# An opening on un-normed x: norms computed beside the products, unread products on TensorE, and a reordered set of loads

## The chip, the cores and the metric

The kernel runs on one core of a Trainium2 chip. The core has five engines that run side by side, each with its own queue of instructions: TensorE (PE in the profile; it multiplies and transposes), VectorE (DVE), ScalarE (ACT), GpSimd (POOL) and SyncE (SP, which here only issues transfers). ACT and POOL can issue transfers too. Sixteen DMA engines carry all transfers. The metric is the device time of one execution in microseconds (us).

## The reference

The reference is one decoder layer on x of 512 tokens by 2048 channels, all in float32:

```
h    = x * rsqrt(mean(x^2) + eps) * g_pre                    # RMSNorm per token
[q | k | v | z_att | u | g_glu | z_conv] = h @ w_in          # 2048 x 7168
A: 8 heads of stick-breaking attention on q, k, v, times silu(z_att)
B: u * sigmoid(g_glu) -> causal depthwise conv (31 taps) -> LayerNorm -> silu
   -> @ w_pw2, times silu(z_conv)
out  = x + RMSNorm(concat(A, B) @ w_out) * g_post
```

Only the first two lines concern the change: the norm of x, and the first 512 of the columns g_glu of the product h @ w_in, which the kernel computes first.

## The kernel before, in words

**Split numbers.** Every float32 operand of a product is split into hi (rounded to the format TensorE multiplies in) and lo (the rest), and a product is made of three: hi x hi, hi x lo, lo x hi. ACT makes hi (`AF.Copy`), DVE makes lo by a subtraction (`split`, lines 99 to 103). A split of a weight block of 128 x 2048 elements takes one ACT and one DVE instruction; in the opening the blocks are split in four parts of 512 columns (`part`).

**The opening** makes the first 512 columns of g_glu by rows: the output is four tiles `ps0[m]` (128 tokens each), and the sum over 2048 channels goes in four groups kg of 512 channels. So there are 16 blocks (kg, m), numbered n = 4 kg + m, each of twelve products of 128 x 512 (`rows_block`, lines 448 to 462; the last four, on line 460, use the low part of x). A block needs the weight group kg (`w0[kg]`, loaded by `load_w0`, hi and lo) and the transposed x tile (m, kg). `turn_x` transposes a tile of x on TensorE (line 244), ACT copies hi out of PSUM (line 248), DVE subtracts lo (line 251), and ACT copies the raw transposed values (line 255, or 250 for kg 0), which later steps use.

**The norm before.** For kg 0 x is used un-normed, with g_pre's 512 factors multiplied into the weight rows; after these blocks `scale_up` multiplies each `ps0[m]` by its token's root. For kg 1 to 3 `scale_x` multiplies x by root and g_pre on DVE (line 231) before it is transposed. For that, g_pre is spread over the 128 partitions by `broadcast_g`: three pairs of products with the constant `pick` (lines 168, 169), each copied to SBUF by DVE. The sums of squares are made by ACT and DVE (`square`), the roots by ACT's Ln and Exp and a Newton step on DVE. The transposed copies of kg 0 are normed at the end by `norm_first`: the roots are spread by four transpositions (`broadcast_roots`), and four steps multiply 512 columns each and split them again.

**The order of work.** In the opening the order on PE, DVE and ACT is written out by hand: the dictionary `plan` lists for each block n (slot n in the text) what is issued ahead of the block and behind it. Transfers on SP and POOL are placed by the planner of the framework, in order of the program's priorities; an instruction that waits holds up those behind it on its queue. A buffer of the pools `raws`, `his` and `los` exists twice, so the third weight group is loaded when the first one's raw tile has been split.

**After the opening** come steps of 1024 x 256 weights, two per pair of 128 output columns: first u (here in the order second half, first half of the channels), then q, k, then v. `stream` loads the raw weights on SP (line 311) and splits them. After u's first step `turn_gates` transposes the four kept row tiles (`keep_rows`) of g_glu on PE, and ACT applies the sigmoid. v is computed by a scheme with seven instead of eight products, for which weight blocks are added in DRAM: `v_sum`, 16 transfers of 1 MB on POOL's queue (lines 484 and 488), from DRAM to DRAM, of which `sum_next` releases one after each block from 5 on and then one after each unit of a step, in order; a sum also waits for the transfer whose result it reads. The depthwise convolution runs on DVE in the background from u's first step on.

Of the kernel before, what the change touches and what calls it, by code (L numbers as in the profile page):

```python
# [48 lines left out]
def hybrid_layer(  # L49
# [81 lines left out]
    pick = const.tile([4, 4, P], F32R, name="pick")  # L131
    for j in range(4):
        nc.gpsimd.tensor_copy(pick[:, j, :], ident[:4, j : j + 1].to_broadcast([4, P]))
# [15 lines left out]
    g_ks = early.tile([4, P], F32, name="g_ks")  # L149
    g_col = const.tile([P, 4], F32, name="g_col")  # L150
    g_rows = t2("g_rows")[:4]
    g_bc = {}

    def turn_g():

        ps = trp.tile([P, S], F32, tag="tr", name="g_col_ps")
        nc.tensor.transpose(ps[:, :4], g_ks, ident[:4, :4])
        nc.vector.tensor_copy(g_col, ps[:, :4])

    def split_g():  # L160
        g_parts = [t2(f"g_{part}", F32R)[:4] for part in ("hi", "lo")]
        split(*g_parts, g_rows)
        return g_parts

    def broadcast_g(j, g_hi, g_lo):

        ps = trp.tile([P, S], F32, tag="tr", name=f"g_ps{j}")
        nc.tensor.matmul(ps, pick[:, j, :], g_hi, start=True, stop=False)
        nc.tensor.matmul(ps, pick[:, j, :], g_lo, start=False, stop=True)
        g_bc[j] = t2(f"g_bc{j}")  # L170
        nc.vector.tensor_copy(g_bc[j], ps)
# [28 lines left out]

    def square(m, j, eng=None):
        junk = t2(f"junk{m}_{j}")
        total = sums[m][:, j : j + 1]
        if eng is None:
            nc.scalar.activation(junk, xts[m][j], AF.Square, accum_out=total)
        else:
            eng.tensor_tensor_reduce(
                out=junk, in0=xts[m][j], in1=xts[m][j], scale=1.0, scalar=0.0,
                op0=ALU.mult, op1=ALU.add, accum_out=total,
            )  # L210
# [3 lines left out]
    def root_table(m):  # L214
# [6 lines left out]
        rsqrt_table(y, v)  # L221
        roots[m] = y, v

# [15 lines left out]
    def turn_x(m, j):  # L239
# [8 lines left out]
        nc.scalar.activation(hi, src, AF.Copy)  # L248
        if j == 0:
            nc.scalar.copy(raw_h[m, 0], src)  # L250
        nc.vector.tensor_tensor(out=lo, in0=src, in1=f32(hi), op=ALU.subtract)

        def keep_raw():
            raw_h[m, j] = t2(f"xw{m}_{j}").rearrange("p (i t) -> p i t", i=4)
# [22 lines left out]
    def norm_first():  # L277

        lo = {}
        for i in range(5):  # L280
            if i < 4:
                x, hi = whole[:, i, :], h_hi[0][:, i, :]
                nc.vector.scalar_tensor_tensor(
                    out=x, in0=x, scalar=g_col[:, i : i + 1], in1=rbc[0],
                    op0=ALU.mult, op1=ALU.mult,
                )
                nc.scalar.activation(hi, x, AF.Copy)
            if i > 0:
                nc.vector.tensor_tensor(
                    out=h_lo[0][:, i - 1, :], in0=whole[:, i - 1, :], in1=f32(h_hi[0][:, i - 1, :]),  # L290
                    op=ALU.subtract,
                )
# [40 lines left out]
    def pair(c0, post, name, halves=(0, 1)):  # L333
# [3 lines left out]
        def unit(half, i):  # L337
            def go(w):
                hi, lo = w
                if half == halves[0]:  # L340
                    ps[i] = mm(f"{name}_{i}")
                cs = slice(i * P, (i + 1) * P)
                for k in range(8):
                    mm3(
                        ps[i], (hi[:, k, cs], lo[:, k, cs]), h_at(half * 8 + k),
                        half == halves[0] and k == 0, half == halves[1] and k == 7,
                    )
                if half == halves[1]:
# [3 lines left out]
        for half in halves:  # L352
# [658 lines left out]
    def conv_in(t):  # L1011
        if t > 1:
            pair(C_G + t * 256, post_g(2 * t), f"g{t}")

        pair(C_U + t * 256, post_u(2 * t), f"u{t}", (0, 1) if t else (1, 0))
# [31 lines left out]
    with tc.manual_schedule(engines={mybir.EngineType.DVE, mybir.EngineType.Activation}):  # L1047
# [5 lines left out]
        def load_w0(kg, eng=nc.sync):  # L1053
            raw, hi, lo = (
                raws.tile([P, 4, S], F32, tag="raw", name=f"r_gn{kg}"),
                his.tile([P, 4, S], F32R, tag="hi", name=f"h_gn{kg}"),
# [210 lines left out]
```

## Time and profile before

| what | value |
|---|---|
| three runs | 877.31 to 878.13 us, median 877.72 us |
| the profiled execution | 880.52 us, its span 878.8 us |
| granted TensorE clock, mean | 0.992 of full |
| PE busy | 856.1 us, 97% of the span |
| DVE / ACT / POOL busy | 625.1 / 391.5 / 123.8 us |
| moved by DMA | 163.32 MB, mean 186 GB/s |

The profile shows one execution. A line such as "start, duration, engine, line, operation, out<-in, shape" is one instruction or several alike in a row (xN); in brackets behind it stands how long the engine had been idle and what released it. PE's matmuls overlap, so the distance from one start to the next is what one costs. In tables of stretches the columns after the time are the busy time of PE, PE's weight loads, DVE, ACT and POOL with their counts, then the granted clock of TensorE, the mean busy share of the DMA engines and their GB/s.

### The profile page before, as it was taken

To read this page: it belongs to the slowest core of one execution; us is meant where nothing else is said; L and a number is where in the kernel's file an instruction comes from. 1 tells how busy PE (TensorE), PEld (TensorE's weight loads), DVE (VectorE), ACT (ScalarE), POOL (GpSimd) and SP (SyncE) were. 2 spreads that over 40 slices of the span, in tenths; PEclk is the share of its full clock that TensorE was granted. 3 is DMA by queue.
4 is the path that set the end of the run, shared out by engine and by line. 5 is a ranking of instruction groups with operands and counts; after the bars stand their busy time and mean duration, and the time that the engine had idled before them with its cause. 6 is when DMAs were issued, how large, how long until landed. Compare 5 with 4: busy or idle time off the path is not lost.

```text
span 878.8 us, 9764 instructions
## 1 busy us (share of the span) xinstructions
PE 856.1 (97%) x3879; PEld 708.3 (81%) x3879; DVE 625.1 (71%) x744; ACT 391.5 (45%) x446; POOL 123.8 (14%) x156
## 2 busy tenths in 40 slices
PE   6899989999999999999999999999999999999995
PEld 4688868888888888888888888888888888888884
DVE  5766877996598987969697994226533676458775
ACT  5653323645434454334432535325823346456543
POOL 0011110001122042213111143122001000000031
PEclk9999989999999999999999999999999999999998
DMA  8499984557776655885477656772233246556783
GB/s 300 160 268 275 290 201 142 192 191 268 247 156 152 183 178 135 186 202 197 156 142 165 192 172 159 166 182 90 78 117 99 96 148 242 193 196 244 290 282 103
DMA packets 87406, 163.32 MB, mean 186 GB/s; under 512 B 2994, under 2 KB 52406, under 8 KB 83584
## 3 DMA queue, kind: packets, MB, share of 16 engines
q1 hardware_dynamic: 70176, 110.92, 37.5%
q0 software_dynamic: 16320, 50.33, 25.2%
q10 hardware_dynamic: 864, 1.44, 0.5%
q8 instruction: 30, 0.49, 0.2%
q14 instruction: 16, 0.13, 0.0%
HBM read 158.49 MB, written 54.53 MB: 242 GB/s over the span
## 4 chain that ended last, share of the span: by engine, by line
PE 89%; DMA 6%; DVE 2%; ACT 2%; issue 0%; DVEq 0%; SPq 0%; ACTq 0%
PE k L328 3%; PE k L326 3%; PE k L327 3%; PE za L327 3%; PE za L326 3%; PE za L328 3%; PE zc L327 3%; PE zc L328 3%; PE a L922 3%; PE a L923 3%; PE zc L326 3%; PE a L924 3%; DMA r_q<-in_w_in_dram 3%; DMA r_k<-in_w_in_dram 3%; PE q L328 2%; PE u L327 2%
## 5 line engine op out<-in xcount | busy, mean ns | idle before, releaser
L383 DVE SCALAR_TENSOR_TENSOR acc<-hg,vec,acc 128x512 f32<-128x512 f32 x240 | 182.3, 759 | 6.9
L100 DVE TENSOR_TENSOR l_w<-r_w,h_w 128x2048 fp32r<-128x2048 f32 x28 | 64.1, 2291 | 42.5 <-ACT h_w L99 42.5
L99 ACT ACTIVATE h_w<-r_w 128x2048 fp32r<-128x2048 f32 x28 | 53.5, 1915 | 42.7 <-DMA r_w<-ws 12.6
L328 PE MATMUL k<-h_hi,l_k 128*128 128x512 f32 x128 | 51.2, 400 | 1.6 <-DVE l_k L100 1.6
L326 PE MATMUL k<-h_hi,h_k 128*128 128x512 f32 x128 | 51.2, 400 | 1.4 <-ACT h_k L99 1.4
L327 PE MATMUL k<-h_lo,h_k 128*128 128x512 f32 x128 | 50.8, 397 | 0.0
L326 PE MATMUL u<-h_hi,h_u 128*128 128x512 f32 x128 | 50.2, 392 | 0.0
L326 PE MATMUL q<-h_hi,h_q 128*128 128x512 f32 x128 | 50.1, 391 | 0.0
L326 PE MATMUL za<-h_hi,h_za 128*128 128x512 f32 x128 | 49.9, 390 | 0.0
L328 PE MATMUL u<-h_hi,l_u 128*128 128x512 f32 x128 | 49.9, 390 | 0.0
L326 PE MATMUL zc<-h_hi,h_zc 128*128 128x512 f32 x128 | 49.9, 390 | 0.0
L328 PE MATMUL q<-h_hi,l_q 128*128 128x512 f32 x128 | 49.9, 390 | 0.0
L327 PE MATMUL u<-h_lo,h_u 128*128 128x512 f32 x128 | 49.9, 390 | 0.0
L327 PE MATMUL q<-h_lo,h_q 128*128 128x512 f32 x128 | 49.9, 390 | 0.0
L328 PE MATMUL za<-h_hi,l_za 128*128 128x512 f32 x128 | 49.8, 389 | 0.0
L327 PE MATMUL za<-h_lo,h_za 128*128 128x512 f32 x128 | 49.8, 389 | 0.0
L328 PE MATMUL zc<-h_hi,l_zc 128*128 128x512 f32 x128 | 49.8, 389 | 0.0
L327 PE MATMUL zc<-h_lo,h_zc 128*128 128x512 f32 x128 | 49.8, 389 | 0.0
L922 PE MATMUL a<-h_w,f_hi 128*128 128x512 f32 x128 | 49.8, 389 | 0.0
L923 PE MATMUL a<-l_w,f_hi 128*128 128x512 f32 x128 | 49.8, 389 | 0.0
L924 PE MATMUL a<-h_w,f_lo 128*128 128x512 f32 x128 | 49.8, 389 | 0.0
L653 POOL TENSOR_SCALAR_AFFINE_SELECT t<-t 128x128 f32<-128x128 f32 x64 | 35.6, 635 | 81.9 <-DVE t L676 48.9
(339 smaller groups left out, 2118.4 us busy)
## 6 DMA issues: line engine op xcount, KB each, us to landing
ws<-in_w_out_dram POOLq DMA_DIRECT2D x24, 1024.0 KB, 9.3
r_w<-ws SPq DMA_DIRECT2D x16, 1024.0 KB
vs<-in_w_in_dram POOLq DMA_DIRECT2D x12, 1024.0 KB, 13.2
r_w<-in_w_out_dram SPq DMA_DIRECT2D x12, 1024.0 KB
r_u<-in_w_in_dram SPq DMA_DIRECT2D x8, 1024.0 KB
r_q<-in_w_in_dram SPq DMA_DIRECT2D x8, 1024.0 KB
r_k<-in_w_in_dram SPq DMA_DIRECT2D x8, 1024.0 KB
r_v<-vs SPq DMA_DIRECT2D x8, 1024.0 KB
```

Source lines behind the costliest of these rows:

```text
L99: nc.scalar.activation(hi, src, AF.Copy)
L100: nc.vector.tensor_tensor(out=lo, in0=src, in1=f32(hi), op=ALU.subtract)
L326: nc.tensor.matmul(ps, wh, ah, start=first, stop=False)
L327: nc.tensor.matmul(ps, wh, al, start=False, stop=False)
L328: latest[0] = nc.tensor.matmul(ps, wl, ah, start=False, stop=last).ins
L383: bgq.append(lambda j=j: nc.vector.scalar_tensor_tensor(out=acc, in0=hg[:, j : j + S], scalar=vec[:, ct, j : j + 1], in1=acc, op0=ALU.mult ...
L653: nc.gpsimd.affine_select(out=blk, in_=blk, compare_op=ALU.is_gt, fill=0.0, base=0, pattern=[[-1, P]], channel_multiplier=1,)
L922: nc.tensor.matmul(ps, fh[:, kk, ts], hi[:, k, :], start=st, stop=False, skip_group_check=True)
L923: nc.tensor.matmul(ps, fh[:, kk, ts], lo[:, k, :], start=False, stop=False, skip_group_check=True)
L924: nc.tensor.matmul(ps, fl[:, kk, ts], hi[:, k, :], start=False, stop=en, skip_group_check=True)
```

## The change

1. *Un-normed x for three groups.* kg 0, 1 and 2 use x as loaded; `g_col` now holds 1536 factors of g_pre (12 x 128 instead of 4 x 128, loaded on ACT's queue), and `part` multiplies them into the weight rows for kg < 3. Only kg 3 is still scaled ahead of its transposition. `scale_up` moves from after group 0 to after group 2. Three of the four spreads of g_pre by products fall away with `pick`, `split_g` and `broadcast_g`; the last 512 factors come spread by one transfer (`load_g(3)`).
2. *Norms beside the products.* Squares, roots and their spread move to slots 1 to 9. `norm_first` now norms three groups of raw copies: group 1 (four tiles of 128 tokens, four multiplications of 128 columns each), group 0 (four multiplications of 512 columns), group 2 (as group 1), each item followed by ACT's hi and DVE's lo; 14 calls instead of 5.
3. *Unread products.* 10 products of a constant into an unread tile before `turn_g`, 3 after it, 8 between the transpositions of the first tile and block 0.
4. *First tile.* For tile (0, 0) hi is copied by DVE instead of ACT, and its lo comes after the four weight parts.
5. *Loads.* The rows of the first weight group are issued on SP, between the x tiles, instead of on ACT's queue; then x by columns; the third and fourth weight group on POOL's queue (slots 3 and 4) instead of SP's; the convolution's vectors at slot 6 instead of 10.
6. *The end.* u's first step is split in slot 13 instead of 12, the second one right after the fourth of the last calls of `norm_first`; u's halves come in the order first, second, with the channels of each half taken from its fifth group of 128 on. `turn_gates` moves ahead of u's first step and takes its 16 transpositions token tile by token tile.

```
+    def root_sum(m):
...
-        nc.scalar.activation(hi, src, AF.Copy)
-        if j == 0:
-            nc.scalar.copy(raw_h[m, 0], src)
-        nc.vector.tensor_tensor(out=lo, in0=src, in1=f32(hi), op=ALU.subtract)
+        if (m, j) == (0, 0):
+            nc.vector.tensor_copy(hi, src)
+        else:
+            nc.scalar.activation(hi, src, AF.Copy)
+            nc.vector.tensor_tensor(out=lo, in0=src, in1=f32(hi), op=ALU.subtract)
...
+        def norm(x, i, ts):
+            nc.vector.scalar_tensor_tensor(
+                out=x, in0=x, scalar=g_col[:, i : i + 1], in1=rbc[0][:, ts],
+                op0=ALU.mult, op1=ALU.mult,
+            )
+        def by_tokens(j, m):
+            x, ts = raw_h[m, j], slice(m * P, (m + 1) * P)
+            for i in range(4):
+                norm(x[:, i, :], 4 * j + i, ts)
+            return h_hi[j][:, :, ts], h_lo[j][:, :, ts], x
+        def by_channels(j, i):
+            x = whole[:, i, :]
+            norm(x, i, slice(0, S))
+            return h_hi[j][:, i, :], h_lo[j][:, i, :], x
+        todo = [(f, j, n) for j, f in ((1, by_tokens), (0, by_channels), (2, by_tokens)) for n in range(4)]
...
+                    k = n if c0 != C_U else (n + 4) % 8
...
-            split(hi[:, i], lo[:, i], raw[:, i], g_col[:, i : i + 1] if kg == 0 else None)
+            k = kg * 4 + i
+            split(hi[:, i], lo[:, i], raw[:, i], g_col[:, k : k + 1] if kg < 3 else None)
...
-        nc.sync.dma_start(g_ks, g_pre[: 4 * P].rearrange("(k p) -> k p", p=P))
+        nc.scalar.dma_start(g_ks, g_pre[: 12 * P].rearrange("(k p) -> k p", p=P))
         load_x(0, 0)
-        load_w0(0, nc.scalar)
-        nc.sync.dma_start(g_rows, g_pre.rearrange("(j c) -> j c", j=4))
-        for m in range(1, NT):
-            load_x(m, 0)
-        load_x(0, 1, 2, 3)
-        load_x(1, 1, 2, 3)
+        load_w0_rows(0)
+        load_w0_rows(1)
+        load_x(1, 0)
+        load_w0_rows(2)
+        load_w0_rows(3)
+        load_x(2, 0)
+        load_x(3, 0)
+        for m in range(NT):
+            load_x(m, 1)
         load_w0(1)
-        load_x(2, 1, 2, 3)
-        load_x(3, 1, 2, 3)
+        for m in range(NT):
+            load_x(m, 2, 3)
+        load_g(3)
+        def idle_products(count):
+            for i in range(count):
+                nc.tensor.matmul(idle[:, :P], mean_w, mean_w, start=True, stop=True)
+        idle_products(10)
         turn_g()
+        idle_products(3)
...
+            1: [do(square, 0, 0), do(square, 2, 0, dve), do(square, 1, 0), do(square, 3, 0, dve)],
+            2: [do(part, 1, 0), do(part, 1, 1), do(square, 0, 1), do(square, 1, 1, dve)],
+            3: [
+                do(load_w0, 2, nc.gpsimd), do(part, 1, 2), do(part, 1, 3),
+                do(square, 2, 1), do(square, 3, 1, dve),
+            ],
...
+            9: [
+                do(part, 3, 1), broadcast_roots, do(scale_block, 12), do(scale_up, 0),
+            ],
+            10: [do(part, 3, 2), do(scale_block, 13), do(scale_up, 1), do(next, first)],
+            11: [do(part, 3, 3), do(scale_block, 14), do(scale_up, 2), do(next, first)],
+            12: [do(scale_block, 15), do(next, first), do(scale_up, 3), do(next, first)],
+            13: [lambda: loaded.update({0: steps[0].load()}), do(keep_rows, 0)],
+            14: [do(keep_rows, 1), do(next, first), do(next, first)],
+            15: [do(keep_rows, 2), do(next, first)],
         turn_block(0)
+        idle_products(8)
         for i in range(4):
             part(0, i)
-        turn_block(1)
-        for m in range(NT):
-            square(m, 0, dve)
+        keeps[0]()
...
         keep_rows(3)
-        next(first)
-        next(first)
+        for _ in range(4):
+            next(first)
+        loaded[1] = steps[1].load()
+        for _ in first:
+            pass
```

More of the change, by code (lines that the diff above doesn't have):

```diff
@@ L156, in turn_g, with load_g @@
         ps = trp.tile([P, S], F32, tag="tr", name="g_col_ps")
[L157 to L169, printed above, removed]
+        nc.tensor.transpose(ps[:, :12], g_ks, ident[:12, :12])
+        nc.vector.tensor_copy(g_col, ps[:, :12])
+    def load_g(j):
         g_bc[j] = t2(f"g_bc{j}")
-        nc.vector.tensor_copy(g_bc[j], ps)
+        nc.sync.dma_start(g_bc[j], g_pre[j * S : (j + 1) * S].partition_broadcast(P))
     NV = TAPS + 4
@@ L1222, in hybrid_layer @@
             sum_next(sumq)
-        if n + 1 < len(steps):
+        if n + 1 < len(steps) and n + 1 not in loaded:
             loaded[n + 1] = steps[n + 1].load()
@@ L1228, in hybrid_layer @@
             sum_next(v_sumq)
-            if n == 0 and unit is step.units[-1]:
-                turn_gates()
             if n == 0 and unit is step.units[0]:
```

184 lines of the change are left out of this document (84 added, 100 removed).

## The prediction, on record before the result

> **What bounds the kernel now.** I read the page first, then TensorE's waits, then the opening in order of time, then stretches of the transfers.
>
> ```profile
> span 878.8 us, 9764 instructions
> PE 856.1 (97%) x3879; PEld 708.3 (81%) x3879; DVE 625.1 (71%) x744; ACT 391.5 (45%) x446; POOL 123.8 (14%) x156
> ```
>
> TensorE (PE) bounds the kernel, so a change can only pay where PE is idle or at half clock. The view of PE's waits names those places, in total us, number and longest.
>
> ```profile
> PE xT L244 <- DMA x<-in_x_dram: 5.0, 2, 3.6
> PE g_col_ps L157 <- POOL pick L133: 2.3, 1, 2.3
> PE xT L244 <- DVE x L231: 2.1, 2, 1.3
> PE k L328 <- DVE l_k L100: 1.6, 1, 1.6
> PE k L326 <- ACT h_k L99: 1.4, 1, 1.4
> PE g_ps L169 <- DVE g_lo L100: 1.1, 1, 1.1
> ```
>
> Four of the six are in the opening, which the change rewrites. The two at k lie at 115 us, and the change doesn't touch them by name. The opening in order of time (start, duration):
>
> ```profile
> 6.13 1.12 PE L244 MATMUL xT<-ident,x 128*128 128x128 f32 x4 [3.59 <-DMA x<-in_x_dram]
> ...
> 8.24 2.56 ACT L102 ACTIVATE h_gn<-r_gn,g_col 128x512 fp32r<-128x512 f32 x4
> ...
> 8.68 2.19 PE L244 MATMUL xT<-ident,x 128*128 128x128 f32 x8 [1.43 <-DMA x<-in_x_dram]
> ...
> 10.52 0.78 PE L453 MATMUL gn<-h_gn,h_hi 128*128 128x512 f32 x1
> ...
> 13.16 1.09 PE L460 MATMUL gn<-h_gn,h_lo 128*128 128x512 f32 x4
> ...
> 26.24 1.08 PE L460 MATMUL gn<-h_gn,h_lo 128*128 128x512 f32 x4
> ...
> 29.44 1.09 PE L460 MATMUL gn<-h_gn,h_lo 128*128 128x512 f32 x4
> ...
> 42.21 1.07 PE L460 MATMUL gn<-h_gn,h_lo 128*128 128x512 f32 x4
> ...
> 45.40 1.09 PE L460 MATMUL gn<-h_gn,h_lo 128*128 128x512 f32 x4
> ...
> 67.83 1.07 PE L460 MATMUL gn<-h_gn,h_lo 128*128 128x512 f32 x4
> ```
>
> The L460 group is the end of a block; the rows are blocks 0, 3, 4, 7, 8 and 15 of 16. From block 7 to 15 PE is dense: (67.83 - 42.21) / 8 = 3.20 us a block, a transposition included. Blocks 0 to 3 take 13.08 where three at 3.20 would be 9.60, and blocks 4 to 7 take 12.77. So the opening holds 10.52 us before the first product, 3.5 us of loss in blocks 1 to 3 and 3.2 in blocks 5 to 7.
>
> **The start.** What has come in by when follows from the stretches (after the brackets: PE clock, share of the DMA engines, GB/s).
>
> ```profile
> 0.00:2.00 2.00, 0.00 (x0) 0.00 (x0) 0.00 (x0) 1.20 (x1) 1.37 (x12) 1.00 0.09 10
> 2.00:4.00 2.00, 0.23 (x1) 0.18 (x1) 0.16 (x1) 0.09 (x1) 0.66 (x3) 1.00 0.80 196
> 4.00:6.00 2.00, 0.00 (x0) 0.00 (x0) 0.00 (x0) 0.00 (x0) 0.00 (x0) 1.00 0.92 231
> 6.00:8.00 2.00, 1.12 (x4) 0.72 (x4) 0.00 (x0) 0.71 (x2) 0.00 (x0) 1.00 1.05 406
> 8.00:10.00 2.00, 1.32 (x5) 0.96 (x6) 1.61 (x3) 2.00 (x4) 0.00 (x0) 1.00 0.97 335
> 10.00:14.00 4.00, 4.00 (x16) 3.35 (x16) 3.95 (x9) 4.00 (x10) 0.00 (x0) 1.00 0.94 284
> 14.00:18.00 4.00, 2.93 (x14) 1.89 (x12) 4.00 (x11) 1.53 (x4) 0.00 (x0) 1.00 1.04 388
> 18.00:24.00 6.00, 6.00 (x28) 4.26 (x26) 5.09 (x17) 3.93 (x12) 0.00 (x0) 1.00 1.02 377
> 35.00:45.00 10.00, 8.71 (x43) 6.72 (x44) 7.79 (x15) 6.18 (x12) 2.83 (x3) 1.00 0.65 209
> 45.00:114.00 69.00, 69.00 (x332) 57.11 (x330) 49.81 (x69) 27.00 (x39) 10.69 (x12) 1.00 1.02 270
> ```
>
> Summed, 0.41 MB are in by 4 us, 0.87 by 6, 1.69 by 8, 2.36 by 10, 3.49 by 14, 5.05 by 18 and 7.31 by 24. Block 0 needs one tile of x and four rows of the weight, 0.26 MB each; the second x makes 1.57 MB. Those were in at 7.7 us, and the second x released PE at 8.68, so a landing shows 1.0 us after its bytes.
>
> Now the first x comes at 6.13, because the ACT queue's weight rows share the engines with it. After, it is alone in front: 0.26 MB at 3.2, landed at 4.2. The last row is sixth in line: 8.7 instead of just under 10. From there the chain is ACT's copy and VectorE's (DVE) rest, then, new, DVE's rest of the first x behind them.
>
> ```profile
> L251 DVE TENSOR_TENSOR h_lo<-xT,h_hi 128x512 fp32r<-128x512 f32 x16 | 11.0, 689 | 16.5 <-ACT h_hi L248 10.8 <-ACT whole L250 5.6
> L231 DVE SCALAR_TENSOR_TENSOR x<-x,y,g_bc 128x512 f32<-128x512 f32 x12 | 8.9, 745 | 0.1
> L103 DVE SCALAR_TENSOR_TENSOR l_gn<-r_gn,g_col,h_gn 128x512 fp32r<-128x512 f32 x4 | 2.7, 746 | 0.0
> L114 DVE SCALAR_TENSOR_TENSOR t<-y,v 128x1 f32<-128x1 f32 x4 | 0.9, 214 | 0.0
> ```
>
> 8.7 + 0.65 (2.56 / 4) + 0.75 + 0.69 = 10.8: block 0's L460 group there instead of 13.16, gain 2.4. Bounds: no landing lag, 9.8 (3.4); rows arriving as late as now, copies done at 10.80 and rests at 12.2 (1.0). I take the middle, by the lag seen.
>
> The unread products aren't in this trace. The nearest row is the four cold transpositions of 128 columns in 1.12 us: ten cost up to 2.8 from about 1.8 us, when their operand is ready, so to 4.6, and turn_g, three more and the transpositions end near 6.7; eight more end between 7.6 (half that price) and 8.9. The first product stands there, 1.6 to 2.9 before today's. Block 0's end is set by the data, so they cost nothing; without them its twelve products could run at half clock, 0.2 us each, 2.4 at most.
>
> The Trainium skill, "TensorE: Matmul & The Clock Gate", part 1, says that the clock opens after about 3.4 us of sustained work and closes after an idle window of that length. By that rule it is open before block 0. No run here shows a filled opening; after the restart at k (rows below) the half clock lasted 5.1 us.
>
> **Blocks 1 to 7.** Gone are the six products that broadcast g (the 1.1 us wait is one of theirs) and the scaling of x ahead of the transpositions of blocks 4 to 11 (the 2.1 us wait). Blocks 1 to 3 need x and raw copies only; ACT and DVE have some 2.5 us of work in each 3.20 us. Gain 13.08 - 9.60 = 3.5. Bounds: 0 if ACT and DVE still trail, and this; I take it, since every named wait goes.
>
> Block 4 needs the second weight block. Its place on SP makes 4.19 MB ahead of and with it: in at 15.8, landed at 16.8. But the third weight block, now on POOL's queue, starts at about 11, when block 0's raw tile is free, and shares: with all of it ahead, 5.24 MB, in at 18.5, landed at 19.5. ACT stands in that wait with two parts, a square, a raw copy and only then block 4's hi copy (some 2.6 us); block 4 would start at 10.8 + 9.6 + 0.9 = 21.3. So the wait is 0 to 0.8; I take 0.5.
>
> The Trainium skill, "DMA: Bandwidth & Descriptors", "Issuing engines are not separate DMA queues", speaks against this edit: transfers from SP, ACT and POOL interleave on the same 16 engines, and a second issuer saves only issue time. By that rule the wait is the 0.8, and the sum below 0.3 less; without sharing it would be 0.5 more.
>
> The fourth group stands on POOL behind the third, until the second one's raw tile is split at about 23, and ahead of the sums, whose first is due at 28: a us of issue each (0.87 for a sum, below), price 0. On SP the vectors' ten small loads now stand at slot 6, ahead of u's, which wait for their raw tile until slot 7: 0 again.
>
> Blocks 5 to 7: 12.77 - 9.60 = 3.2 gained, 0 if the chain of the roots still held up ACT; I take it, as no transposition waits for a root any more until block 12, whose scaling stands three blocks ahead.
>
> **Blocks 8 to 15.** They are dense now; nothing to gain. DVE loses eight scalings (L231) and three copies of g, and gains eight rests of 0.69 and 32 multiplications of 128 columns. The latter has no row: between 0.21 (one column) and 0.75 (512 columns); by line 0.35, I take that. For slots 10 to 15 I count on DVE six rests of x, two of weights, three scalings, seven steps of norm_first and one split of u at some 2.3, together about 18 us in 19.6: hidden by PE's products, with 1.5 to spare. Without that cover the first product of u waits for the same time that DVE is over; 2 us at the upper price.
>
> The transpositions of the gates move from the second step of u to before the first: same work, moved. They need the last kept rows, one ACT copy of about 0.6 after block 15, behind twelve transpositions that don't. Price 0. Sixteen transpositions ahead also give norm_first that time.
>
> Sum at the first product of u: 2.4 + 3.5 - 0.5 + 3.2 = 8.6, bounds 4 and 10.
>
> **Where the time could be given back: k.** The chain of waits, then PE's order of time:
>
> ```profile
> 62.24 25.11 DMA r_q<-in_w_in_dram
> ...
> 91.72 22.69 DMA r_k<-in_w_in_dram
> ```
> ```profile
> 114.68 0.39 PE L328 MATMUL q<-h_hi,l_q 128*128 128x512 f32 x1
> ...
> 119.39 0.63 PE L326 MATMUL k<-h_hi,h_k 128*128 128x512 f32 x1
> ...
> 124.09 0.63 PE L328 MATMUL k<-h_hi,l_k 128*128 128x512 f32 x1
> 124.52 0.48 PE L326 MATMUL k<-h_hi,h_k 128*128 128x512 f32 x1
> ```
>
> The last row is the 16th product of k. Dense, at 0.227 from 114.91, it would start at 118.3, so k costs 6.2 us, 2.4 of them the twelve from 119.39 to 124.09 at half clock. The weight is late because the DMA engines are full from 45 to 114 (1.02): 1 MB takes 22.7 us beside the sums of v's weights on POOL. If those transfers stayed where they are, all 8.6 would become idle time here. They don't: the sums are released by blocks.
>
> ```profile
> 35.11 0.87 POOL L488 DMA_DIRECT2D vs<-in_w_in_dram  x1 [32.46 <-PE gn L460]
> ```
>
> The first comes right after block 5, the next three after 6 to 8, which move by 7 (block 5 is early in the recovery) to 8.6 us; the next ones follow on landings. The engines are only 0.65 busy from 35 to 45, so 3.5 us more can be taken up. The loads of u go by when their raw tile is free, also 6 to 9 earlier. The split of u's first half moves back by one slot, so q's first load is issued only about 5 us earlier, but it stands behind u's second half, which is about 8.7 earlier. I expect k's weight 8 to 9 us earlier and the 6.2 kept. Bounds: moved by 4 only (4.6 given back) and by 15 (6.2 more gained).
>
> The profiled execution took 880.52, 1.72 around its span: 880.52 - 8.6 = 871.9. It lay 2.8 above the median of 877.72; carried over, 869.1.
>
> **Rivals.** (1) The transfers follow PE only partly: k's wait, or q's, which has little slack, takes back 3 to 6 us: 872 to 875; at worst all, 877.7. For it: engines at 1.02 and the later split; against: everything that feeds the queue is released by PE's blocks. (2) The transfers gain more than PE, for they can fill the idle share before 45: k's wait shrinks, 863 to 866. The skill's clock page has the gate close only after a window of 3.4 us idle; here two gaps of 1.4 and 1.6 closed it, so the trace differs, and by the rule the 2.4 would be saved as well. (3) Slower: the second weight block comes last. ACT and DVE take it in order in slots 2 and 3, ahead of the hi copies of blocks 4 and 5, so each us past a landing at 18.7 (21.3 less 2.6) costs PE one, and over 3 us of idleness a half clock again, 2.4. Without any wait the gain is 9.1, so the kernel is slower from a landing at 25.4 on (6.7 + 2.4). All opening bytes, 7.34 MB, are landed at 25 by today's stretches; with x's last columns and the third weight block all ahead of it, and a rate 10% lower, it lands at 27.5: 8.8 + 2.4 - 9.1 = 2.1 slower, 879.8. Against: it is queued on SP ahead of those columns. (4) The change doesn't do what it says: the data comes no earlier, 1.0 instead of 2.4 at the start: 870.5; with DVE over by 2: 872.5.
>
> **Numbers.** Forecast 0.64 (866.5 to 871.5), (1) 0.14, of it 0.05 within 0.2%, (2) 0.10, (3) 0.05, (4) beyond the forecast 0.07. The time is 869.1. The range, 864.0 to 874.0, leaves out about 0.07 of (1), all of (3) and 0.03 of (2). A measurement tells 0.2%, 1.8 us, from no change: faster 0.90, same 0.05, slower 0.05.
>
> **What would show it.** Block 0's L460 group near 10.8, block 3's near 20.4, block 7's near 33.6, block 15's near 59.2; no wait of L244 on DVE; the first sum on POOL near 28; k's two waits still there, with PE at half clock for some 5 us after. The forecast is wrong if q or k waits over 5 us, if PE idles over 2 us ahead of block 4, or if u's first products wait for h_lo.

## The result and the profile after

| | before | after |
|---|---|---|
| median, 5 runs each on one chip | 877.31 us (873.92 to 878.13) | 871.03 us (868.98 to 871.51) |
| the profiled execution, its span | 880.52, 878.8 us | 871.51, 869.8 us |

The ratio is 0.9941, with a 95% interval of 0.9917 to 0.9966: faster, by 6.3 us between the medians. Before's five times fall apart, 873.92 and 873.94 against 877.31 to 878.13, so the 6.3 hangs on which of them is the median; the section on the prediction returns to it. The forecast was 869.1 us, in a range of 864.0 to 874.0. First the page of the kernel after, the span and the busy time of the engines, then its view of TensorE's waits (total us, number, longest).

```profile
span 869.8 us, 9834 instructions
PE 855.0 (98%) x3894; PEld 710.0 (82%) x3894; DVE 631.0 (73%) x773; ACT 395.3 (45%) x452; POOL 124.5 (14%) x154
```
```profile
PE va L635 <- DVE l_v L100: 2.4, 1, 2.4
PE idle L1123 <- POOL mean_w L134: 1.8, 1, 1.8
PE k L344 <- DVE l_k L100: 1.1, 1, 1.1
PE va L634 <- ACT v_a L596: 0.4, 1, 0.4
```

All waits of the opening are gone but the one ahead of the first unread product (line 1123), which holds up unread products alone. k keeps one of its two waits. On top stands a wait that before didn't have, in v; the last row, 0.4 us, lies in v too. TensorE in order of time, after (lines 471, 472 and 478 are before's 453, 454 and 460; line 237 is the transposition):

```profile
5.93 1.95 PE L1123 MATMUL idle<-mean_w 128*128 128x128 f32 x8
7.67 0.73 PE L471 MATMUL gn<-h_gn,h_hi 128*128 128x512 f32 x1
...
9.91 0.63 PE L472 MATMUL gn<-l_gn,h_hi 128*128 128x512 f32 x1
10.34 0.55 PE L471 MATMUL gn<-h_gn,h_hi 128*128 128x512 f32 x1
10.73 0.39 PE L472 MATMUL gn<-l_gn,h_hi 128*128 128x512 f32 x1
...
11.43 1.08 PE L478 MATMUL gn<-h_gn,h_lo 128*128 128x512 f32 x4
...
21.06 1.09 PE L478 MATMUL gn<-h_gn,h_lo 128*128 128x512 f32 x4
...
24.27 1.09 PE L478 MATMUL gn<-h_gn,h_lo 128*128 128x512 f32 x4
...
33.92 1.09 PE L478 MATMUL gn<-h_gn,h_lo 128*128 128x512 f32 x4
...
59.62 1.07 PE L478 MATMUL gn<-h_gn,h_lo 128*128 128x512 f32 x4
...
60.53 2.17 PE L1212 MATMUL gT<-ident,g_nat 128*128 128x128 f32 x16
62.45 0.48 PE L342 MATMUL u<-h_hi,h_u 128*128 128x512 f32 x1
```

The five L478 groups of four are the ends of blocks 0, 3, 4, 7 and 15. From block 0 on every block takes 3.21 us: the opening is dense. Its end moved from 67.83 to 59.62, by 8.2 us. But block 0 itself still runs at half clock: products start 0.43 apart (9.91 to 10.34) until about 10.7, and 0.23 apart after (10.73 to 10.96). The column of the granted clock reads 1.00 throughout the opening (it reads 0.50 at k in the first profile of before, 119.4 to 124.0), so in the opening the clock is read from the distance of the products.

Then k and v. First the two loads from the chain of waits of after; then single rows in order of time of ScalarE, VectorE and TensorE.

```profile
58.12 19.88 DMA r_q<-in_w_in_dram
82.38 21.91 DMA r_k<-in_w_in_dram
```
```profile
104.39 1.92 ACT L99 ACTIVATE h_k<-r_k 128x2048 fp32r<-128x2048 f32 x1 [17.24 <-DMA r_k<-in_w_in_dram]
106.34 2.29 DVE L100 TENSOR_TENSOR l_k<-r_k,h_k 128x2048 fp32r<-128x2048 f32 x1 [4.44 <-ACT h_k L99]
108.68 0.50 PE L344 MATMUL k<-h_hi,l_k 128*128 128x512 f32 x1 [1.11 <-DVE l_k L100]
130.20 6.26 DVE L401 SCALAR_TENSOR_TENSOR acc<-hg,vec,acc 128x512 f32<-128x512 f32 x8
136.38 2.28 DVE L100 TENSOR_TENSOR l_v<-r_v,h_v 128x2048 fp32r<-128x2048 f32 x1
138.72 0.50 PE L635 MATMUL va<-l_v,h_hi 128*128 128x512 f32 x1 [2.41 <-DVE l_v L100]
```

k's high part starts at 104.39, 10.1 earlier than the 114.51 of before's profile, more than TensorE gained. So k is reached at full clock with one wait instead of two. (Against the second profile of before, in experiment e0, k's high part is not earlier: there it starts at 104.06.) In v, VectorE has eight convolution taps of 6.26 us ahead of the low part of v's next weights, and TensorE stands for 2.41. A table of stages follows: where TensorE's first product of each stage starts, in the order of time of five profiles. "Before, second" is the profile of experiment e0; e3 and e10 are kernels of the experiments.

| first product of | before | before, second | after | e3 | e10 |
|---|---|---|---|---|---|
| q | 93.14 | 93.01 | 85.20 | 85.56 | 84.57 |
| k | 116.48 | 114.77 | 106.96 | 107.32 | 106.33 |
| v | 142.98 | 136.53 | 130.48 | 129.08 | 128.09 |
| attention (z) | 224.90 | 218.23 | 215.77 | 210.81 | 210.37 |
| end of the span | 878.8 | 872.2 | 869.8 | 864.9 | 864.4 |

Dense, a pair q or k takes 21.76 us (93.01 to 114.77, and on to 136.53) and the stretch from v to attention 81.70. By that, the profiled execution of before loses 1.58 ahead of k, 4.74 in k and 0.22 from v on: 6.5. After loses 1.76 in k and 3.59 from v on: 5.35. The sum of the pair of profiles: 8.21 in the blocks, less 0.27 from block 15 to q (25.58 instead of 25.31), plus 6.54 - 5.35 = 1.19, less 0.13 from attention on: 9.0, which is 878.8 - 869.8.

### The profile page after: what moved, and what is told of

It reads as the page before. It is cut to its first block, busy times and chain, and to the rows that moved or that the text cites. A ratio compares the mean times of both kernels' runs of the same rounds, so it can differ in the third digit from the quotient of the medians.

```text
span 869.8 us, 9834 instructions
## 1 busy us (share of the span) xinstructions
PE 855.0 (98%) x3894; PEld 710.0 (82%) x3894; DVE 631.0 (73%) x773; ACT 395.3 (45%) x452; POOL 124.5 (14%) x154
## 4 chain that ended last, share of the span: by engine, by line
PE 80%; DVE 10%; DMA 6%; ACT 2%; issue 1%; POOL 0%; DVEq 0%; ACTq 0%; POOLq 0%
PE za L342 3%; PE zc L342 3%; PE za L344 3%; PE a L940 3%; PE zc L344 3%; PE za L343 3%; PE a L942 3%; PE zc L343 3%; PE a L941 3%; DVE acc L401 3%; DVE l_v L100 3%; DMA r_k<-in_w_in_dram 3%; PE k L342 3%; PE q L344 3%; PE q L342 3%; PE u L344 3%
## 6 DMA issues: line engine op xcount, KB each, us to landing
vs<-in_w_in_dram POOLq DMA_DIRECT2D x12, 1024.0 KB, 12.9
```

## The experiments

All twelve were timed in five rounds beside the kernel before on the same chip, four to a chip. Line numbers are those of the kernel named.

### The opening

**e1: no unread products**

```
-        idle_products(10)
         turn_g()
-        idle_products(3)
...
-        idle_products(8)
```

> The changed kernel without its 21 unread products; nothing else differs. Theory A (what the trace of after suggests): they are too thin to open TensorE's clock, since the first twelve products still start 0.43 us apart until about 10.3 us although PE had been busy from 1.8 us on; so without them block 0's last group starts where it did (11.4 us, within 0.5) and the time is the same within 1 us. Theory B (the purpose that the change names): without them the clock opens later and blocks 0 and 1 lose about 2.4 us, twelve products at 0.43 instead of 0.23; the time rises by 2 to 3 us. Theory C: they delay the first product (7.7 us); without them it starts at 6.5 and the end is up to 1 us earlier.

Measured: 870.75 us (869.56 to 872.85), ratio 0.9937 (0.9913 to 0.9961); the kernel after has 0.9941. The first product starts earlier, at 6.91, released by VectorE's copy of x; TensorE, in order of time:

```profile
6.91 0.76 PE L471 MATMUL gn<-h_gn,h_hi 128*128 128x512 f32 x1 [0.88 <-DVE h_hi L242]
```

It stays at half clock until about 12.9, block 0's last group comes at 11.48, and u's first product at 63.20, 0.75 later than after's 62.45. The numbers of theory A held, and the earlier start of theory C, though not its end. The thin unread products hold the first product back by 0.76. That they open the clock sooner is likely but small: in the seven profiles with these products (after, e2 to e5, e8, e11) it opens between about 9.0 and 12.1, here at 12.9. What they bring at u isn't shown: the seven have u at 61.86 to 63.42, and the medians don't differ.

**e7: the same products 512 columns wide**

```
-                nc.tensor.matmul(idle[:, :P], mean_w, mean_w, start=True, stop=True)
+                nc.tensor.matmul(idle.rearrange("p (i t) -> p i t", i=4), mean_w, mean_w.unsqueeze(1).to_broadcast([P, 4, P]), start=True, stop=True)
...
-        idle_products(10)
+        idle_products(5)
...
-        idle_products(3)
+        idle_products(2)
...
-        idle_products(8)
+        idle_products(4)
```

> The kernel after with its unread products 512 columns wide instead of 128 (5, 2 and 4 of them in place of 10, 3 and 8, so that TensorE's share of full work in the same stretch is higher). Theory A (the clock opens by how much the array works, and thin products do not open it): block 0's products come at the full pitch from its first one on, block 0's last group at 10.5 instead of 11.43, u up to 1 us earlier, the median 869.5 to 870.5. Theory B (the clock opens so long after the first busy stretch, whatever its width): half clock until 9.5 to 11.5 as in the runs so far, the first product no earlier, the median 870 to 872.

Measured: 868.92 us (866.89 to 871.83), ratio 0.9917 (0.9884 to 0.9949). TensorE in order of time:

```profile
1.77 2.50 PE L1123 MATMUL idle<-mean_w 128*128 128x512 f32 x5 [1.77 <-POOL mean_w L134]
...
6.03 1.19 PE L1123 MATMUL idle<-mean_w 128*128 128x512 f32 x4
7.15 0.47 PE L471 MATMUL gn<-h_gn,h_hi 128*128 128x512 f32 x1
...
10.49 1.17 PE L478 MATMUL gn<-h_gn,h_lo 128*128 128x512 f32 x4
11.67 0.50 PE L471 MATMUL gn<-h_gn,h_hi 128*128 128x512 f32 x1
```

Four wide products take 1.19, which is the full clock, and block 0's first product 0.47. Theory A held for the clock: with the wide products it opens before block 0, whose last group comes at 10.49, 0.94 earlier than after. u comes at 61.88, 0.57 earlier. The rest goes at the end of block 0, where the next product waits for ScalarE's copy (11.67 - 10.49 = 1.18 for four products that take 0.91). The wide products fix the moment more than they advance u: e10, the other kernel with them, opens the clock at about 6.3 and has u at 61.86, but so have two kernels with thin ones in which it opened early (e5 61.86, e8 61.96). Since the wide products are also more work in all, the run doesn't tell width from amount. The median lies 2.1 below after's, but the two intervals overlap, and this profile has the same waits in k and v as after.

**e6: before, with the new order of the first loads alone**

```
-        nc.sync.dma_start(g_ks, g_pre[: 4 * P].rearrange("(k p) -> k p", p=P))
+        nc.scalar.dma_start(g_ks, g_pre[: 4 * P].rearrange("(k p) -> k p", p=P))
         load_x(0, 0)
-        load_w0(0, nc.scalar)
+        load_w0_rows(0)
+        load_w0_rows(1)
+        load_x(1, 0)
+        load_w0_rows(2)
+        load_w0_rows(3)
```

> The kernel before with one part of the change: the first loads in the new order (the gain vector on ScalarE's queue, the first weight block by single rows on SP's between x's tiles). The normed x, the norms ahead of the products, the gates' place and the idle products stay as they were. Theory A (the opening is bound by x's first tile and its norm, as the wait lines of before say): block 0's last product group starts 0.5 to 2 us earlier than its 13.16, and no more than 2 us of that is left at u; the median is 875 to 877. Theory B (what the change gains is the loads' order, the rest of it is cover): most of the 6.3 us between the medians is here already, 871 to 873.

Measured: 873.46 us (872.98 to 877.62), ratio 0.9989 (0.9969 to 1.0009): not told from no change. TensorE in order of time:

```profile
5.06 1.12 PE L244 MATMUL xT<-ident,x 128*128 128x128 f32 x4 [2.40 <-DMA x<-in_x_dram]
...
13.51 1.39 PE L460 MATMUL gn<-h_gn,h_lo 128*128 128x512 f32 x4
...
68.13 0.39 PE L326 MATMUL u<-h_hi,h_u 128*128 128x512 f32 x1
```

The first tile is there 1.07 sooner (5.06 instead of 6.13), but block 0's last group comes at 13.51; u starts at 68.13 instead of 68.73, or 68.60 in the second profile of before, whose block 0 ends with a group at 13.97. So some 0.5 of the gain is the order of the loads by itself. Eight of the twelve times lie at 872.98 to 874.09, four at 876.19 to 877.62: two groups as in before (on this chip from 873.86 and from 878.58 on), the first some 0.7 lower. Theory A's 0.5 us at block 0 is there against the second profile only, and its 875 to 877 was missed. The larger part of the 8.2 needs the rest of the change, and no run separates its other parts: that the waits of blocks 1 to 3 and 5 to 7 went with the products for g and the scaling of x is seen in the profile, not tested by leaving one of them in. Theory B is out.

**e11: the first tile's high part by ScalarE again**

```
-            nc.vector.tensor_copy(hi, src)
+            nc.scalar.activation(hi, src, AF.Copy)
```

> The kernel after with one part undone: the high part of x's first tile is copied by ScalarE again, not by VectorE. Theory A (VectorE's copy at 6.31 takes a place of 0.69 us ahead of the weights' low parts, and ScalarE is free until the first weight row, at 6.01): block 0's low part and its last group come up to 0.7 us earlier if the rows allow, otherwise ScalarE's copy of 0.6 pushes both weight rows back and the first product moves from 7.67 to about 8.2; at u a difference of under 0.7 either way, the median 870 to 872. Theory B (the copy on VectorE is what lets the first product come so early): block 0's last group at 12.2 or later, the median 872 to 873.

Measured: 871.40 us (870.59 to 872.77), ratio 0.9951 (0.9933 to 0.9968). Block 0's last group is at 12.36 and u at 63.42, 0.97 later than after, but the median is 0.4 above after's and the span the same. Neither theory's numbers hold together. The half clock ended at about 12.1 here and at 10.7 in after, and that moment differs between kernels with the same opening as after's (about 9.7 in e5, 11.6 in e3), so this run doesn't separate the copy from it. It shows something else: TensorE doesn't wait in k here, and waits 2.4 in v all the same.

**e2: third and fourth weight group on SP's queue again**

```
-                do(load_w0, 2, nc.gpsimd), do(part, 1, 2), do(part, 1, 3),
+                do(load_w0, 2), do(part, 1, 2), do(part, 1, 3),
...
-                do(root_sum, 0), do(load_w0, 3, nc.gpsimd),
+                do(root_sum, 0), do(load_w0, 3),
```

> The changed kernel with the third and fourth weight group of the opening on SP's queue instead of POOL's, placed by the planner right behind x's last columns and the spread factors. Theory A: all transfers share the same engines, the opening's loads still land well ahead of their blocks, and the second group even comes earlier; PE stays dense through the opening, u's first product within 0.5 us of 62.45, time the same within 1 us. Theory B: the POOL queue is what keeps the opening dense; the vectors' loads and u's first load, which stand behind the two groups on SP, come later, block 8 or 12 waits for its weights, and u's first product is 1 to 4 us later.

Measured: 870.03 us (865.63 to 872.22), ratio 0.9921 (0.9893 to 0.9950). u comes at 62.79, and k and v wait 0.5 and 2.4 us. The queue of these two loads makes no difference that shows.

### k and v

**e3: POOL's sums from block 7 on**

```
-            if n >= 5:
+            if n >= 7:
                 sum_next(v_sumq)
```

> The changed kernel with the sums of v's weights released from block 7 on instead of block 5, so that each starts two blocks, 6.4 us, later; the opening itself is untouched. Theory A: the engines are full up to k, so k's first load lands 5 to 6 us later than 104.4, that is near 110; PE, which reaches k at 107, waits 5 to 6 us there in place of 1.3 and half the clock follows (2.4); the time rises by 5 to 9 us. Theory B: k's load is late for another reason (its own issue, which waits for the split of q), the sums have slack, and the time rises by less than 1.5 us.

Measured: 866.65 us (865.84 to 867.46), ratio 0.9890 (0.9868 to 0.9913), 4.4 below after's median. Neither theory held: it is neither slower nor the same. The view of TensorE's waits has one row left, and ScalarE in order of time shows why:

```profile
PE idle L1123 <- POOL mean_w L134: 1.8, 1, 1.8
```
```profile
74.71 1.92 ACT L99 ACTIVATE h_q<-r_q 128x2048 fp32r<-128x2048 f32 x1 [0.51 <-PE u L343]
88.44 1.92 ACT L99 ACTIVATE h_q<-r_q 128x2048 fp32r<-128x2048 f32 x1 [9.73 <-DMA r_q<-in_w_in_dram]
96.42 1.92 ACT L99 ACTIVATE h_k<-r_k 128x2048 fp32r<-128x2048 f32 x1 [6.06 <-PE q L343]
```

q's load, issued at 58.49 (after: 58.12), was in when TensorE let ScalarE go on at 74.71, within 16.2 us; after's took until 78.0, 19.9, and in the four other profiles with the sums from block 5 on and the taps as in after (e1, e2, e7, e11) it took 20.6 to 21.1. k's was in by 96.42 instead of 104.3. The two loads are a chain, for k's raw tile is free only when q's is split, and POOL's sums stand beside both on the same DMA engines. SP issues k's load when q's low part is made (78.98 here, 82.38 in after). That is the chain which made k late. v's wait went with it, as VectorE's rows show:

```profile
101.93 2.28 DVE L100 TENSOR_TENSOR l_k<-r_k,h_k 128x2048 fp32r<-128x2048 f32 x1
131.96 2.28 DVE L100 TENSOR_TENSOR l_v<-r_v,h_v 128x2048 fp32r<-128x2048 f32 x1
```

From k's first low part to v's second one VectorE takes 30.0 us, taps and other splits between, here (101.93 to 131.96) as in after (106.34 to 136.38), e1, e2, e7 and e11. So a late start at k is handed on to v: after's is 4.4 later at both ends.

**e4: POOL's sums from block 3 on**

```
-            if n >= 5:
+            if n >= 3:
```

> The kernel after with POOL's sums released from block 3 on instead of block 5. Theory A (the sums take the loads of q and k their share of the DMA engines, so what counts is how many stand beside these loads): two sums more stand in front of them, k's weight lands later than 104.3, k waits 2 to 5 us and the half clock follows, the median 872 to 876. Theory B (sums that are done before block 7 are out of the way of q's and k's loads later): k's wait is gone as with the sums from block 7, 866 to 868.

Measured: 867.39 us (866.14 to 869.69), ratio 0.9908 (0.9883 to 0.9933). No wait in k or v. ScalarE in order of time:

```profile
75.00 1.92 ACT L99 ACTIVATE h_q<-r_q 128x2048 fp32r<-128x2048 f32 x1 [0.90 <-DMA r_q<-in_w_in_dram]
...
99.35 1.92 ACT L99 ACTIVATE h_k<-r_k 128x2048 fp32r<-128x2048 f32 x1 [11.97 <-DMA r_k<-in_w_in_dram]
```

Theory B's numbers held: two blocks earlier is about as good as two later. So a release earlier or later isn't what hurts; the load of q took 16.6 us here (58.40 to 75.00), 19.88 in after. That it depends on which stretch of the sums falls on q's load fits the three release points, but no run isolates it.

**e5: half as many convolution taps in k's last two steps**

```
-                background(1 if n_v <= n < n_att else 4, LATER)
+                background(1 if n_v <= n < n_att else 2 if n_v - 2 <= n < n_v else 4, LATER)
```

> The changed kernel with half as many taps of the background convolution placed on VectorE during k's two steps (2 instead of 4 per unit); the taps come later, none is left out. In VectorE's order the split of v's second weight half then stands ahead of eight taps instead of behind them. Theory A: the 2.4 us that PE waits in v at 138.7 us in the trace of after is VectorE's own backlog, because PE came 12.5 us earlier to v and VectorE only some 9; without the taps ahead the wait is gone and the time falls by 2 to 2.8 us. Theory B: the wait only moves (a later split of v, or the taps that come later hold up u's next pair), and the time is the same within 1 us.

Measured: 867.23 us (866.14 to 867.91), ratio 0.9895 (0.9871 to 0.9920), 3.8 below after's median. The wait in v is gone, as theory A had it. In this profile k's wait is gone too, and u came 0.59 sooner (61.86), so not all of the 3.8 is shown to be the taps'. The wait in v is: k's first low part starts at 103.90 and v's second at 130.05, 26.2 us later. By the 30.0 of the full taps it would have started at 133.9, 5.8 after v's first product (128.12); in after it started 5.9 behind it, and TensorE waited 2.4 (an estimate from these rows).

**e9: before, with POOL's sums from block 7 on**

```
-            if n >= 5:
+            if n >= 7:
```

> The kernel before with POOL's sums held until block 7 instead of block 5, nothing else. Theory A (k's two waits in before, 1.4 and 1.6, and the half clock behind them come of the sums standing beside the loads of q and k): both waits are gone, 5 to 7 us, 870 to 873, and the opening is as long as in before (block 15's last product group at 67.8). Theory B (in before the loads come late because the whole opening is late, and there is room enough for the sums): under 2 us, 875 to 878.

Measured: 874.03 us (873.88 to 874.25, 12 runs), ratio 0.9981 (0.9962 to 0.9999). Theory A had the waits right and the size wrong; theory B's size held (under 2 us) and not its reason. k's waits are gone, and yet the time is only that of the better executions of before. On the same chip the unchanged kernel gave 17 times between 873.86 and 874.62 and 6 between 878.58 and 880.36, with nothing in between. So the edit took the second group away and left the first where it was.

**e0: the kernel before, profiled a second time**

> The kernel before itself, unchanged, for a second profile of it, since its times fall into two heaps, near 874.0 and near 878.5. Theory A (the heaps differ by the waits at k and the half clock behind them): a profiled execution near 875.8 shows no half clock in k's first products and a wait of under 2 us, one near 880 shows twelve products at half clock, as the one shown. Theory B (they differ somewhere else, in the opening or after z): k's first products look the same in both.

Measured: 874.26 us (873.89 to 878.84, 12 runs: 8 up to 874.32, 4 from 877.21 on), ratio 0.9999 (0.9979 to 1.0019). The profiled execution took 873.89. Its view of TensorE's waits:

```profile
PE xT L244 <- DMA x<-in_x_dram: 4.8, 2, 3.4
PE g_col_ps L157 <- DMA g_ks<-in_g_pre_dram: 2.4, 1, 2.4
PE xT L244 <- DVE x L231: 2.1, 2, 1.3
```

No wait in k, no half clock: theory A held. What made the difference is k's load. SP's and ScalarE's rows in order of time, first of this second profile:

```profile
90.89 0.37 SPq L311 DMA_DIRECT2D r_k<-in_w_in_dram  x1
104.06 1.92 ACT L99 ACTIVATE h_k<-r_k 128x2048 fp32r<-128x2048 f32 x1 [7.36 <-PE q L328]
```

then of the first, and the stretch 92 to 96 us of both (the last three columns are granted clock, share of the DMA engines, GB/s), the first profile's row standing first:

```profile
91.72 0.37 SPq L311 DMA_DIRECT2D r_k<-in_w_in_dram  x1
114.51 1.91 ACT L99 ACTIVATE h_k<-r_k 128x2048 fp32r<-128x2048 f32 x1 [17.73 <-DMA r_k<-in_w_in_dram]
```
```profile
92.00:96.00 4.00, 4.00 (x19) 3.32 (x18) 3.75 (x6) 1.89 (x3) 2.18 (x3) 1.00 0.90 150
```
```profile
92.00:96.00 4.00, 4.00 (x20) 3.30 (x19) 3.82 (x6) 1.22 (x1) 2.08 (x3) 1.00 1.02 310
```

The load that SP issued 0.83 us sooner was in within 13.2 us; the other took 22.7. POOL issued its next sum at 90.69 and 90.62, an issue of 1.17 us: one load came 0.20 after its start, the other 1.10, near its end. That the place of the load among that sum's packets decides fits both profiles, but is only argued.

### The edits together

**e8: sums from block 7, and half the taps** (the diffs of e3 and e5)

> The kernel after with both edits that helped alone: POOL's sums held until block 7 instead of block 5, and half as many convolution taps on VectorE in k's last two steps. Theory A (both take away the same thing, TensorE's waits for k's and v's second halves, and each alone left none of these): nothing on top of the better one, 866 to 867.5. Theory B (they act on different things, the loads' share of the DMA engines and VectorE's queue ahead of the low part): they add, 863 to 865.

Measured: 866.72 us (866.28 to 867.41), ratio 0.9897 (0.9870 to 0.9925). Nothing on top of either alone: theory A. No wait in k, and in v 0.3 us.

**e10: e8 with the wide unread products** (the diffs of e3, e5 and e7)

> The kernel after with three edits together: unread products 512 wide (5, 2, 4), POOL's sums from block 7 on, half the taps in k's last two steps. Theory A (each loss has its own cause: the wide products open the clock before block 0, the two others take away the waits at k and v): u's first product at 61.9 in every execution, no wait at k or v, and the median 0.5 to 1 us below the 866.7 of the sums and taps alone, 865.5 to 866.3. Theory B (the moment at which the clock opens in block 0 is made good later, in the norms beside the blocks): 866.4 to 867, as without the wide products.

Measured: 866.26 us (866.18 to 866.46), ratio 0.9893 (0.9871 to 0.9915). The view of TensorE's waits, and u's first product:

```profile
PE idle L1123 <- POOL mean_w L134: 1.8, 1, 1.8
PE va L634 <- ACT v_a L596: 0.4, 1, 0.4
```
```profile
61.86 0.48 PE L342 MATMUL u<-h_hi,h_u 128*128 128x512 f32 x1
```

It is the fastest of all, ahead of both kernels, and its six times lie within 0.3 us. Against e8 the median gained 0.5, on another chip, which is less than such a comparison can carry.

## Why the prediction was right, and where it was not

**The opening: right.** Block 15's last group was forecast at 59.2 and came at 59.62. By terms: the start gained 1.73 where 2.4 was forecast; blocks 1 to 3 3.45 (3.5); block 4's wait for the second weight group 0 (0.5 lost); blocks 5 to 7 3.12 (3.2); blocks 8 to 15 -0.08 (0). Together 8.2 for 8.6. How the first two share the gain hangs on when the clock opens (block 0's last group stands at 13.97 in the second profile of before, and at 10.61 in e8, whose opening is after's). Their sum hangs on it by under a microsecond (u comes at 61.86 to 62.81 in the six profiles with after's unread products and first tile). The first sum on POOL was issued at 28.88 (28), and no transposition waits for VectorE. u's first product is 6.28 earlier and not 8.6, because the gates' transpositions, 2.17, now stand in front of it; at q, with the gates behind both, the gain is 7.94. The stretch from block 15 to q, which holds them in both kernels, grew by 0.27 where 0 was forecast.

**Block 0, the mis-sized term.** "Block 0's end is set by the data, so they cost nothing" failed. The products ran at half clock until 10.7 and set the end at 11.43; with the clock open (e7) the same data allowed 10.49. The forecast's 10.8 was near what the data allow. The Trainium skill, "TensorE: Matmul & The Clock Gate", part 1, has the clock open after about 3.4 us of sustained work. After's thin products kept TensorE occupied from 1.76 on and the clock opened 8.9 us later, in the six other profiles with them 7.2 to 10.4; with wide ones it was open at 6.03, 4.3 us after the first. So the rule nearly fits the wide products and not the thin ones. What the kernel loses without any of them was bounded by 2.4; e1 has u 0.75 later than after, within the range that kernels with the thin products show (61.86 to 63.42), so a loss isn't shown.

**VectorE's cover: right.** u waits for nothing after the gates. The multiplication of 128 columns, priced at 0.35, takes 0.26 (four in 1.05, in the chain of waits):

```profile
48.97 1.05 DVE xw L280 x4
```

**k: right against the profile that was priced, wrong against the other one, and wrong in what follows.** k's weight was to come 8 to 9 us earlier "and the 6.2 kept". SP issued its load 9.3 earlier than in the first profile of before (82.38 and 91.72) and 8.5 earlier than in the second (90.89). It was in 10.1 earlier than in the first, so k lost 1.76, without the half clock, as rival (2) had it. In the second it was in by 104.06, so against that one after's (104.39) gained nothing, while TensorE reaches k 7.8 earlier (106.96 and 114.77). And then v lost 3.59, for which no case had a term. The sum of the losses, 5.35 for 6.2, is near by luck, because one took the other's place.

What the runs show of v: VectorE's taps stand ahead of l_v in before too. But there l_v starts 2.8 after v's first product (139.29 and 136.53, second profile), in e3 2.9 (131.96 and 129.08), in after 5.9 (136.38 and 130.48). Where v doesn't wait, VectorE starts k's first low part well ahead of k's first product: 5.2 us in the second profile of before (109.56 and 114.77), 5.4 in e3 (101.93 and 107.32). In after it is 0.6 ahead (106.34 and 106.96). In e11 it is 2.4 ahead (105.54 and 107.92), which is enough for k and not for v. So VectorE was behind by its wait for k's late load, and its queue should have been asked what is late next. Against the second profile of before, e3, which has none of these losses, gains 7.3 (872.2 - 864.9), about what its q gained (93.01 - 85.56 = 7.45).

**The carry-over from profile to median: wrong.** "It lay 2.8 above the median of 877.72; carried over, 869.1" took the offset for a constant. After's profile lies 0.5 above its median. Over all runs the unchanged kernel was timed 73 times: 45 times 873.84 to 874.62, and 28 times 877.19 to 880.36. The profiled execution belongs to the second group, and so do the three times behind 877.72; what parts 880.5 from 877.7 within that group stays open, for no execution near 877.7 was profiled. The 6.2 us that were "kept" are nearly the whole difference between the groups' profiles (878.8 - 872.2 = 6.6). So the pair of profiles differs by 9.0 (8.6 forecast), the medians by 6.3, and the forecast missed 871.03 by 1.9. Against the first and larger group, at about 874.0, the change is worth 3.0 us; against the second about 7. That before's median came from the second group again is luck. After isn't one time either: kernels with its sums and taps ran at 865.63 (e2) and 866.89 (e7) at best, and only one execution of after was profiled.

**The rivals.** (1) gave the time nearly (872 to 875). Against the first profile of before its cause wasn't there, for the transfers more than followed; against the second it was: k's weight came no earlier, and of the 8 us of the opening 5.35 were lost again. (3) didn't happen: block 4 starts without a wait, and in e2 the queue of the later weight groups has no effect that shows. (4) had its number, 0.7 less at the start, and not its cause: the data came, and the clock was late.

By the rule of the Trainium skill, "DMA: Bandwidth & Descriptors", "Issuing engines are not separate DMA queues", block 4 would have waited 0.8. It didn't wait; but after against e3 and e4, where shifting POOL's sums alone shortens SP's load of q by 3 us and more, fits the page's statement that the two share the engines.

## What to carry to other kernels

Ask whether the profiled execution is a typical one before pricing a loss from it: here times in two groups meant that one wait was there or not, and a second profile found it. When a stage moves, the loads and the background transfers behind it meet in another phase, so try the release point of the background work on both sides (here 4 us, more than the change itself brought against the larger group of before's times). And when a load comes late, follow the engine that works on it to its next deadline: here the wait at k was 1.1 us and the one that it left behind in v 2.4. Unread products should be looked at in the trace: here 128 columns wide they left the first products of block 0 at half clock, 512 wide they didn't.

## What the runs showed of the hardware that was not expected

- Unread products of 128 columns cost 0.24 us each (eight in 1.95) and left the clock half for 8.9 us in after, 7.2 to 10.4 in six other profiles; 512 wide it opened in 4.3 (e7) and 4.5 (e10).
- A pause of 2.4 us in v closed the clock in three of five profiles with it (e1, e7, e11), not in after and e2. In e1 the column of the granted clock reads 0.50 from 140 to 142 us. The group of lines of e1 and of after, products of v between 100 and 160 us (busy, mean ns | idle):

```profile
L635 PE MATMUL va<-l_v,h_hi 128*128 128x512 f32 x16 | 7.1, 444 | 2.4 <-DVE l_v L100 2.4
```
```profile
L635 PE MATMUL va<-l_v,h_hi 128*128 128x512 f32 x16 | 6.4, 397 | 2.4 <-DVE l_v L100 2.4
```

- The same 1 MB load took at most 13.2 us in one profile of before and 22.7 in the other, issued 0.83 us later beside the same sums.
